# Row-by-row transfers for two early loads and the first store of an RMSNorm + SiLU kernel

**Chip and metric.** One core of one Trainium2 chip. The metric is the time of one execution on the device in microseconds (us).

## The reference

```python
batch, seq_len, hidden = 8, 1024, 2048            # x: 64 MB of float32, gamma: 2048
rms = np.sqrt(np.mean(x ** 2, axis=-1, keepdims=True) + eps)
out = gamma * x / rms
return (out * (1 / (1 + np.exp(-out)))).astype(np.float32)
```

## The kernel before

The engines go by the profile's names: PE multiplies matrices, DVE and ACT compute on vectors, SP only issues transfers here. A transfer (one `dma_start`) is cut into packets, which 16 DMA engines move (from 5 to 300 us 16.04 packets are open on the mean, by the packet records); a packet here is one contiguous run of 2 to 32 KB (a block's load is 128 packets of 32 KB, one a partition). When a transfer has landed, its completion semaphore says so, and that is what others wait on: load 0's was complete at 13.10, and the waits of ACT and DVE on it stand in the trace at 13.12 and 13.13.

The 8192 rows are cut into 16 blocks of 128 partitions x 4 rows (4 MB each, 32 KB in a partition). Six block buffers go round. Loads are issued from SP's queue, stores and gamma's 8 KB load from ACT's. The parts that matter:

```python
    J = 4
    BUFS, LEAD = 6, 6
...
    def load(b):
        xt = pool.tile([P, J * d], f32, name="xt")
        nc.sync.dma_start(out=xt, in_=xb[b])
        blocks[b] = xt
...
    def store(b):
        nc.scalar.dma_start(out=ob[b], in_=blocks[b])
        if b + LEAD < nblk:
            load(b + LEAD)
...
        grow = pool.tile([P, J * d], f32, name="xt")       # gamma's tile, one of the six buffers
        for b in range(BUFS - 1):
            load(b)                                        # loads 0 to 4
...
        nc.scalar.dma_start(out=grow[0:P:P // Q, 0:w], in_=...)   # gamma, on ACT's queue
        ...                                                # PE spreads gamma, DVE copies it to g
        load(BUFS - 1)                                     # load 5, into gamma's buffer
        ...
        sums(0)        # DVE squares rows 2 and 3, ACT rows 0 and 1
        invert(0)
        finish(0)      # DVE multiplies by 1/rms and g, ACT applies silu
        sums(1)
        invert(1)
        for b in range(1, last - 1):
            sums(b + 1, after_first=[b - 1])               # store(b - 1) is issued in here
            finish(b)
            invert(b + 1)
```

## Time and profile before

| | before |
|---|---|
| time, median of 3 runs | 317.5 us (317.2 to 317.74) |
| DVE and ACT busy | 71% each |
| loads + stores, share of 16 DMA engines | 49.7% + 49.2% |
| load 0 landed / store 0 issued / store 0 landed | 13.1 / 36.67 / 61.4 us |
| load 4 / load 5 landed | 64.6 / 84.0 us |
| last store issued / landed | 304.8 / 315.3 us |

The trace is of one further execution, which took 318.03 us.

The page's rows of slices cut the span into 40; the DMA row gives the busy share in tenths. A landing time here is the arrival of a transfer's completion in the trace. The prediction shows the lines themselves.

### The profile page before, as it was taken

How to read it: one execution, taken by the hardware profiler on the slowest of the kernel's cores; microseconds unless marked ns; L12 is line 12 of the kernel's file. 1: busy time of each engine (PE TensorE's matmuls, PEld its weight loads, DVE VectorE, ACT ScalarE, POOL GpSimd, SP SyncE). 2: the span in 40 equal slices, each digit the busy share in tenths (PEclk: the TensorE clock that was granted, in tenths of full speed). 3: DMA queues.
4: the chain of work that ended last, by engine and by line, in shares of the span. 5: the costliest groups of instructions: out<-in, count | busy, mean ns of one | idle time of the engine just before them, and what ended most of it. 6: DMA issues, size and time to landing. Idle time of an engine off the chain costs nothing.

```text
span 316.3 us, 444 instructions
## 1 busy us (share of the span) xinstructions
PE 2.1 (1%) x8; PEld 0.5 (0%) x8; DVE 223.5 (71%) x147; ACT 223.8 (71%) x144; POOL 0.2 (0%) x4
## 2 busy tenths in 40 slices
PE   0200000000000000000000000000000000000000
PEld 0000000000000000000000000000000000000000
DVE  0679499999493983939849397593966939993900
ACT  1357958999967777678676687676786776879540
POOL 0000000000000000000000000000000000000000
DMA  8999999999999999999999999999999999999996
GB/s 328 402 464 410 452 390 410 452 419 443 439 424 452 411 452 410 452 414 456 406 456 414 448 414 448 439 423 452 414 452 410 452 414 456 406 456 410 452 407 269
DMA packets 4763, 134.25 MB, mean 425 GB/s; under 512 B 532, under 2 KB 532, under 8 KB 536
## 3 DMA queue, kind: packets, MB, share of 16 engines
q1 hardware_dynamic: 2304, 67.11, 49.7%
q10 hardware_dynamic: 2456, 67.12, 49.2%
q14 instruction: 3, 0.02, 0.0%
HBM read 67.12 MB, written 67.11 MB: 424 GB/s over the span
## 4 chain that ended last, share of the span: by engine, by line
DMA 74%; DVE 14%; ACT 5%; issue 2%; DVEq 1%; ACTq 0%; SPq 0%
DMA xt<-in_x_dram 44%; DMA out_dram<-xt 30%; DVE xt L84 11%; ACT xt L88 3%; DVE junk_v L64 3%; ACT junk_a L68 1%; DVEq L164 1%; ACT L74 0%; ACT rms L74 0%; DVE rstd L79 0%; ACTq L93 0%; DVE ss L64 0%; SPq L52 0%; DVEq L64 0%; ACTq L74 0%
## 5 line engine op out<-in xcount | busy, mean ns | idle before, releaser
L84 DVE SCALAR_TENSOR_TENSOR xt<-xt,rstd,g 128x2048 f32<-128x2048 f32 x64 | 146.2, 2347 | 0.1
L88 ACT ACTIVATE xt<-xt 128x4096 f32<-128x4096 f32 x32 | 115.4, 3615 | 36.8 <-DVE xt L84 36.7
L64 DVE CUSTOM_DVE_ANT_0 junk_v<-xt 128x2048 f32<-128x2048 f32 x32 | 73.5, 2298 | 56.1 <-DMA xt<-in_x_dram 55.5
L68 ACT ACTIVATE junk_a<-xt 128x2048 f32<-128x2048 f32 x32 | 60.1, 1879 | 29.2 <-DMA xt<-in_x_dram 28.3
L74 ACT ACT_TABLE_LOAD x15 | 19.2, 1283 | 9.9 <-DVE ss L64 9.9
L88 ACT ACT_TABLE_LOAD x15 | 19.2, 1283 | 3.1 <-DVE xt L84 2.9
L79 DVE RECIPROCAL rstd<-rms 128x4 f32<-128x4 f32 x16 | 2.8, 172 | 11.3 <-ACT rms L74 11.3
L114 DVE COPY g<-junk_v 128x2048 f32<-128x2048 f32 x1 | 2.3, 2292 | 9.2 <-PE junk_v L112 9.2
L68 ACT ACTIVATION_READ_ACCUMULATOR junk_a<-xt 128x1 f32 x32 | 6.0, 186 | 0.0
L74 ACT ACTIVATE rms<-ss,eps_t 128x4 f32<-128x4 f32 x16 | 4.8, 297 | 1.2 <-DVE ss L64 1.1
L64 DVE DVE_READ_ACCUMULATOR2_ANT ss<- 128x1 f32 x32 | 4.5, 141 | 0.0
L112 PE MATMUL junk_v<-xt,ones 1*128 1x512 f32 x8 | 2.1, 1133 | 8.1 <-DMA xt<-in_gamma_dram 8.1
L107 ACT ACT_TABLE_LOAD x1 | 1.3, 1283 | 0.7 <-PEq L150 0.7
L105 DVE MEMSET ones<- 128x128 f32 x1 | 0.2, 165 | 0.8 <-PEq L150 0.8
L112 PEld LDWEIGHTS junk_v<-xt,ones 1*128 1x128 f32 x8 | 0.5, 306 | 8.1 <-issue 8.1
L107 ACT ACTIVATE junk_a<-ones 128x1 f32<-128x1 f32 x1 | 0.2, 174 | 0.0
L150 POOL MEMSET const-uint8-127<- 128x1 uint8 x1 | 0.1, 102 | 0.0
L150 POOL MEMSET const-bfloat16-1.0<- 128x1 bf16 x1 | 0.1, 101 | 0.0
L150 POOL MEMSET const-float32-0.0<- 128x1 f32 x1 | 0.1, 98 | 0.2 <-issue 0.2
L150 POOL MEMSET const-float32-1.0<- 128x1 f32 x1 | 0.1, 98 | 0.0
L106 DVE MEMSET eps_t<- 128x1 f32 x1 | 0.1, 59 | 0.0
## 6 DMA issues: line engine op xcount, KB each, us to landing
xt<-in_x_dram SPq DMA_DIRECT2D x16, 4096.0 KB, 42.0
out_dram<-xt ACTq DMA_DIRECT2D x15, 4096.0 KB, 35.2
out_dram<-xt ACTq DMA_DIRECT2D x2, 2048.0 KB, 10.4
xt<-in_gamma_dram ACTq DMA_DIRECT2D x1, 8.0 KB
```

The costliest lines, as they stand in the source:

```text
L64: nc.vector.tensor_tensor_reduce(out=junk_v, in0=row(b, j), in1=row(b, j), scale=1.0, scalar=0.0, op0=ALU.mult, op1=ALU.add, accum_out=ss[ ...
L68: nc.scalar.activation(out=junk_a, in_=row(b, j), func=ACT.Square, accum_out=ss[:, j:j + 1])
L74: nc.scalar.activation(out=rms, in_=ss, func=ACT.Sqrt, scale=1.0 / d, bias=eps_t)
L79: nc.vector.reciprocal(out=rstd, in_=rmss.pop(b))
L84: nc.vector.scalar_tensor_tensor(out=row(b, j), in0=row(b, j), scalar=rstds[b][:, j:j + 1], in1=g, op0=ALU.mult, op1=ALU.mult)
L88: nc.scalar.activation(out=blocks[b][:, cols], in_=blocks[b][:, cols], func=ACT.Silu)
L105: nc.vector.memset(ones, 1.0)
L107: nc.scalar.activation(out=junk_a[:, 0:1], in_=ones[:, 0:1], func=ACT.Square)
L112: nc.tensor.matmul(junk_v[:, c * w:(c + 1) * w], ones[k:k + 1, :], grow[k:k + 1, 0:w], start=True, stop=True)
L114: nc.vector.tensor_copy(out=g, in_=junk_v)
L150: nc = _bacc.Bacc("TRN2", target_bir_lowering=False, num_devices=1)
L164: with _tile.TileContext(nc) as tc:
```

## The change

Its intent: smaller runs for the transfers that meet at the start, so that the first store and the loads beside it take turns in smaller steps, and a block's rows come in one by one. The bytes and the compute stay the same.

```diff
+    LOADS, STORES = (3, 4), (0,)
...
+    def pieces(single):
+
+        step = d if single else J * d
+        return [slice(c, c + step) for c in range(0, J * d, step)]
+
     def load(b):
         xt = pool.tile([P, J * d], f32, name="xt")
-        nc.sync.dma_start(out=xt, in_=xb[b])
+        for c in pieces(b in LOADS):
+            nc.sync.dma_start(out=xt[:, c], in_=xb[b][:, c])
         blocks[b] = xt
...
     def store(b):
-        nc.scalar.dma_start(out=ob[b], in_=blocks[b])
+        for c in pieces(b in STORES):
+            nc.scalar.dma_start(out=ob[b][:, c], in_=blocks[b][:, c])
```

## The prediction

> **What bounds the kernel now.** I read the page's slices and queues first, then the timeline of the first 60 us and of the end, the waits of the issuing queues, and last the packet records behind the DMA view.
>
> ```profile
> span 316.3 us, 444 instructions
> ...
> DMA  8999999999999999999999999999999999999996
> GB/s 328 402 464 410 452 390 410 452 419 443 439 424 452 411 452 410 452 414 456 406 456 414 448 414 448 439 423 452 414 452 410 452 414 456 406 456 410 452 407 269
> ...
> q1 hardware_dynamic: 2304, 67.11, 49.7%
> q10 hardware_dynamic: 2456, 67.12, 49.2%
> ```
>
> q1 carries the loads, q10 the stores. Together they fill 98.9% of 16 engines' span; only the first and last slice are thin. By the packet records, data moves from 1.7 to 313 us (thinly to 314.9) with one packet at a time on each engine. A 32 KB packet takes 1213 ns, a 16 KB one 611, a 2 KB one 84. A block is 8 such packets per engine, and loads that run alone end 9.68 us apart; 16 blocks in and out are 32 x 9.68 = 309.8 us. So DMA bytes bind, and only idle DMA or dearer packets can change the time much.
>
> ```profile
> 0.73 139.01 SPq L52 DMA_DIRECT2D xt<-in_x_dram  x11
> ...
> 1.03 1.09 ACTq L108 DMA_DIRECT2D xt<-in_gamma_dram  x1
> 2.02 0.17 ACT L107 ACTIVATE junk_a<-ones 128x1 f32<-128x1 f32 x1
> ...
> 8.09 2.09 PE L112 MATMUL junk_v<-xt,ones 1*128 1x512 f32 x8 [8.09 <-DMA xt<-in_gamma_dram]
> 10.24 2.29 DVE L114 COPY g<-junk_v 128x2048 f32<-128x2048 f32 x1 [9.24 <-PE junk_v L112]
> 13.19 1.88 ACT L68 ACTIVATE junk_a<-xt 128x2048 f32<-128x2048 f32 x1 [10.99 <-DMA xt<-in_x_dram]
> 13.24 2.30 DVE L64 CUSTOM_DVE_ANT_0 junk_v<-xt 128x2048 f32<-128x2048 f32 x1 [0.71 <-DMA xt<-in_x_dram]
> ...
> 36.67 0.36 ACTq L93 DMA_DIRECT2D out_dram<-xt  x1
> ...
> 55.81 0.34 ACTq L93 DMA_DIRECT2D out_dram<-xt  x1
> ...
> 69.78 0.34 ACTq L93 DMA_DIRECT2D out_dram<-xt  x1
> ```
>
> In this timeline gamma's 8 KB go out on ACT's queue at 1.03, PE spreads them at 8.09, DVE copies them, and only then does DVE begin block 0 (13.24). The first store follows at 36.67. Until then six loads, 58 us of DMA work, keep the engines full. That cushion is what the start lives on.
>
> ```profile
> L93 ACTq DMA_DIRECT2D out_dram<-xt x4: 338/338/338, 69.8 to 123.4; - x4
> L93 ACTq EVENT_SEMAPHORE  x3: 17/17/17, 84.0 to 123.4; - x3
> ```
>
> These are the stores issued between 60 and 130 us: three of the four have an extra semaphore wait ahead of them, though no data need it. The trace's DMA instructions say why: every transfer names a completion semaphore, and there are eight, taken in turn in program order: 100, 102, 103, 104, 105 for loads 0 to 4, 106 for gamma, 108 for load 5, 109 for store 0, then 100 again for load 6. Store 3 is the next user of 106, and its extra wait is on 106, gamma's. Load 7, next on 103 after load 2, waits for 103 beside store 1's semaphore. So a transfer waits until the previous user of its semaphore has landed. Today that user landed long ago, and the wait takes 17 ns.
>
> [...] 1213 against 611 ns gives 9 ns plus 36.7 ns per KB, so about 310 ns for 8 KB. [...] once store 0 has begun, packets of q1 and q10 alternate. [...] here store 1's issue (55.81) comes as the last silu of block 1 ends, and nothing behind it overtakes it.
>
> **The change, part by part.**
>
> *Packets.* Three blocks go from 8 packets of 1213 ns to 32 of 310 on each engine: 3 x 8 x (4 x 310 - 1213) = 0.65 us at most. The start-to-start pitch is some 3 ns under the duration, so I take 0.5 us.
>
> *Numbering.* Loads 3 and 4 are now eight transfers, so the turns of the eight semaphores move. Loads 0 to 2 take turns 1 to 3, load 3's rows 4 to 7, load 4's first row 8; its other rows take turns 1, 2, 3 again and wait for loads 0, 1, 2 (harmless, the queue is full). **Gamma, the twelfth transfer, takes turn 4 again, and must wait until the first row of load 3 has landed.** That is my main step. Before, gamma was the sixth and waited for nobody.
>
> *When gamma goes.* Load 2 lands at 32.50; a row is 8 packets of about 0.306, 2.45 us, so ACT's queue is released at 34.95 and issues gamma at 35.0. Before, 5.1 us passed from issue to its first packet, of which about 1.2 is latency (load 0 took 1.0) and 3.9, some 3.2 packets of 32 KB, was queueing. Behind 8 KB packets that is about 1.0: first packet at 37.2, landed near 38.0, PE at 38.1, the copy done 4.4 later at 42.5 (8.09 to 12.53 before). DVE begins block 0 at 42.6 rather than 13.24: **29.3 us late**. ACT's squares of block 0, stuck behind the issue, start at 35 and are done before DVE needs them.
>
> *What it costs.* From there to the first store compute waits for no load, so I shift the timeline: stores 0, 1, 2 at 66.0, 85.1, 99.1. Loads: 3 ends at 42, 4 at 51.7, 5 (released when PE has read gamma at 40.2) at 61.4. Then the DMA has nothing.
> - Gap A: from 61.4 to the first store packet, 66.0 + 1.4 = 67.4: 6.0 us.
> - Gap B: store 0 alone runs from 67.4 to 77.2. Load 6 needs its buffer: landed 77.7, issued 77.8, first packet 78.9: 1.7 us.
> - Gap C: load 6 runs nearly alone until 88.6, then store 1 until 98.2; load 7 waits for it, first packet 99.8: 1.6 us.
>
> After that store 2 (99.1), 3 (113) and 4 (127), 14 us apart as compute runs, are ahead of the 19.36 us that a block takes in and out, so neither queue runs dry again. Loads 3 and 4 have long landed when store 0 goes out, so finer interleaving does nothing.
>
> *The end.* Stores lag and loads lead: I get load 14 at 256.7 (258.9 now), so compute (last issue 45.9 us after load 14) isn't the bound, and all lost DMA time stays lost. Sum: 6.0 + 1.7 + 1.6 + 0.5 = 9.8 us. 317.5 + 9.8 = **327.3 us**, 3.1% slower.
>
> **The rivals.**
>
> *No such wait for gamma* (a semaphore is picked by another rule than the turn, or the waits go another way). For it: today's trace shows no such wait between two transfers of different queues. Against it: the order of the eight is the turn throughout, 34 transfers long. Then the compute keeps its times, and the shares decide: store 0's 8 KB packets alternate with load 3's and 4's, but when store 0 is done near 58, about 3.5 us of load 4 is left against store 1's 32 KB packets, which get four fifths of the engines. Load 4 would land some 7 us late, and so the following loads. The end has about 3 us of slack (last store issued 304.8, landing 315.3, against 7.5 us that a half block takes by itself). 318 to 322 us.
>
> *Equal shares and no wait*: only the packets' 0.5 us; 318.0.
>
> *The gaps are smaller*: if gamma got through faster or store 0 came sooner, gap A shrinks one for one, but the 23.4 us of compute from block 0's start to its store stand in the timeline, and B and C are latency. I allow 2 us each way.
>
> *A gain*: the DMA is 98.9% busy and no packet gets cheaper; some 3 us at the two ends are all there is to win. I see no way to 2%.
>
> **Range and chances.** I give the gamma wait 85%, with a spread of about 2 us around 327.3; the rest lies at 318 to 322. Slower by over 2% begins at 323.9: 0.84; within 2% 0.15; faster 0.01. Range 323.5 to 329.5.
>
> **What would show it.** In the changed kernel's timeline gamma's issue stands near 35 instead of 1.03, PE's matmul near 38, DVE's first block near 42.6, store 0's first piece near 66; the slices have a hole near 62 to 67 and thin places near 78 and 99; the waits of ACT's first squares are some 24 us long beyond today's 11; queue shares sum to about 96%. If gamma is issued before 5 us, the main step is wrong. If gamma is late but no hole follows, the cushion of six loads was mis-sized.

In the trace of the kernel before, from 54 to 58 us, 30 packets of q1 stand against 29 of q10. That a transfer waits for the last user of its semaphore was inferred there from a few waits, such as store 3's on 106; the changed kernel and e8 show it below. The 1.2, 1.4 and 1.1 us before a first packet are my estimates (load 0's 1.00 us is what that trace shows on idle engines, and e4 later 0.86), and so are the 0.5 us from a last packet to its landing (0.43 at that kernel's end, from 314.89 to 315.32) and the 7.5 us of a half block (e1's last store took 7.20, from 307.82 to 315.02).

## The result

317.97 us (317.57 to 318.32, 6 runs) against 317.45 us (317.2 to 317.86, 6 runs) for the kernel before. The ratio is 1.0015, 95% interval 1.0002 to 1.0028. A ratio here is the mean time of one kernel's fast runs over that of the other's of the same rounds, so not quite the ratio of the medians. Executions over 1.5% slower than the fastest of the same kernel are left out of the means. The kernel is the same within 2%, and the forecast of 327.3 was wrong.

The page of the changed kernel, span, DMA slices, GB/s and queues:

```profile
span 316.0 us, 463 instructions
...
DMA  8999999999999999999999999999999999999996
GB/s 332 411 453 402 423 422 443 418 446 428 431 432 411 449 423 440 440 427 448 415 448 415 448 415 452 411 452 411 456 406 460 411 452 419 448 441 423 444 409 280
...
q1 hardware_dynamic: 3168, 67.11, 49.7%
q10 hardware_dynamic: 2888, 67.12, 49.3%
```

The DMA row is that of the kernel before: no hole anywhere. The packet counts grew by 864 and 432, which are the small runs (768 and 384 more packets) and the completions of the additional transfers (96 and 48 of 4 bytes). Yet the start of the changed kernel is not that of the kernel before. From its timeline (start, duration, engine, line, operation, and in brackets the idle time before it and what ended it):

```profile
12.96 1.09 ACTq L116 DMA_DIRECT2D xt<-in_gamma_dram  x1
14.09 1.88 ACT L75 ACTIVATE junk_a<-xt 128x2048 f32<-128x2048 f32 x1 [11.90 <-issue]
...
20.35 2.09 PE L120 MATMUL junk_v<-xt,ones 1*128 1x512 f32 x8 [20.35 <-DMA xt<-in_gamma_dram]
22.50 2.29 DVE L122 COPY g<-junk_v 128x2048 f32<-128x2048 f32 x1 [21.50 <-PE junk_v L120]
24.82 2.30 DVE L71 CUSTOM_DVE_ANT_0 junk_v<-xt 128x2048 f32<-128x2048 f32 x1
...
48.25 1.32 ACTq L101 DMA_DIRECT2D out_dram<-xt  x3
```

Gamma is late, as forecast, but at 12.96 and not at 35. By the operands that the trace keeps of each instruction, it waits on semaphore 100, load 0's, which was complete at 12.94. Compute starts 11.6 us later than before (24.82 against 13.24), and so does the first store (48.25 against 36.67). The transfers of both kernels take the eight completion semaphores in these turns, worked out from the semaphore that each transfer names in the trace:

| | turns 1 to 8 | then |
|---|---|---|
| before | loads 0 to 4, gamma, load 5, store 0 | load 6, store 1, ... |
| changed | loads 0, 1, 2, load 3's four rows, load 4's first row | **gamma**, load 4's other rows, load 5, store 0's rows, ... |

So there was a wait and a late start, and the DMA still never ran dry.

### The profile page after: what moved, and what is told of

The parts are those of the page before. It is cut to its first block, busy times and chain, and to the rows that moved or that the text cites. A ratio compares the mean times of both kernels' runs of the same rounds, so it can differ in the third digit from the quotient of the medians.

```text
span 316.0 us, 463 instructions
## 1 busy us (share of the span) xinstructions
PE 2.1 (1%) x8; PEld 0.5 (0%) x8; DVE 223.2 (71%) x147; ACT 223.1 (71%) x144; POOL 0.2 (0%) x4
## 4 chain that ended last, share of the span: by engine, by line
DMA 30%; ACT 21%; DVE 18%; another core or an unknown queue 12%; issue 11%; DVEq 1%; PE 1%; ACTq 0%; SPq 0%
DMA out_dram<-xt 15%; ACT xt L95 13%; DVE xt L91 13%; DMA xt<-in_x_dram 12%; DVE junk_v L71 4%; ACT junk_a L75 3%; DMA xt<-in_gamma_dram 2%; ACT L81 2%; ACT L95 2%; ACT rms L81 1%; DVE g L122 1%; DVEq L172 1%; PE junk_v L120 1%; ACTq L101 0%
## 5 line engine op out<-in xcount | busy, mean ns | idle before, releaser
L71 DVE CUSTOM_DVE_ANT_0 junk_v<-xt 128x2048 f32<-128x2048 f32 x32 | 73.5, 2296 | 36.7 <-DMA xt<-in_x_dram 36.1
```

The lines of the kernel that those rows point to most:

```text
L71: nc.vector.tensor_tensor_reduce(out=junk_v, in0=row(b, j), in1=row(b, j), scale=1.0, scalar=0.0, op0=ALU.mult, op1=ALU.add, accum_out=ss[ ...
```

## The experiments

Each experiment is one kernel, run in turn with the kernel before, whose median was 317.62 us beside e1 to e4, 317.54 beside e5, e6, e7 and e9, and 317.34 beside e8 and e10. Code cuts leave lines out where they show `...`. "Stretched" below is worked out from the trace's packet records: the sum of what all packets took beyond the usual duration of their size (1213, 611 and 309 ns for 32, 16 and 8 KB), divided by 16 engines. It is 1.69 us in the kernel before (0.77 of it at the very start, 0.85 between 37 and 42 us, almost all of it in the loads' packets between store 0's issue at 36.67 and its first packet at 40.76) and 1.38 us in the changed one.

My theory after the result (**the cushion**): gamma waits for the last user of its semaphore, and the six loads, which fill the DMA until about 61 us, hide the late start as long as store 0 goes out before that. **Rivals:** any late start is made up later; a late start costs the 0.5 us; the small packets and their share of the engines cost it.

### e1_rows_no_wait: the small packets without the wait

```diff
-        nc.sync.dma_start(out=xt, in_=xb[b])
+        if b in (3, 4):          # rows 0 and 2, then rows 1 and 3: 8 KB runs, two transfers
+            for k in range(2):
+                nc.sync.dma_start(out=halves(xt, k), in_=halves(xb[b], k))
+        else:
+            nc.sync.dma_start(out=xt, in_=xb[b])
...                               # store 0 alike
```

> Loads 3 and 4 and store 0 in 8 KB packets as in the change, but in two transfers each (rows 0 and 2, rows 1 and 3), so that the eight semaphores suffice for the first eight transfers and gamma waits for nobody. All theories: gamma issued near 1.0 us, DVE begins block 0 near 13.2, store 0 issued near 36.7. Packets only: 0.2 to 0.6 us over the kernel before (about 317.9), load 4 landed near 65 as before. Shares by packet (a 32 KB packet of store 1 for each 8 KB packet of load 4): load 4 landed at 69 to 74 instead of 64.6, the later loads some 5 us late too, and 320 to 322 us, because the end has only about 3 us of slack.

Measured: 317.89 us, ratio 1.0013 (1.0 to 1.0025). Gamma went out at 1.03, and DVE began block 0 at 13.18. The shares are by packet, as the transfers of the window from 62 to 66 us show (packets, MB, share of the engines; q10 has store 1's 32 KB packets, q1 mostly load 4's 8 KB ones):

```profile
q10 hardware_dynamic: 44, 1.41, 81.5%
q1 hardware_dynamic: 42, 0.47, 27.3%
```

About as many packets, three times the bytes. Load 4 landed at 68.3 instead of 64.6 and the last loads 3.05 us late. I had expected 5 us, and 320 us and more from it. Store 0's first packet came 4.4 us after its issue, no sooner than before (4.1), so it ended later, and when store 1's first packet went out at 60.6, 53 packets of load 4 were left, about 1.0 us of all engines' work, where the prediction had 3.5. The last store was issued at 307.82 instead of 304.77 and landed at 315.02 instead of 315.32: the slack at the end took all 3.05 us. So the time alone, which lies where "packets only" had it, would have misled; the landings decide.

### e2, e3, e4: gamma late by a chosen amount, all packets 32 KB

```diff
+        nc.scalar.copy(out=grow[0:1, 0:1], in_=blocks[0][0:1, 0:1])   # e3: blocks[1], e4: blocks[2]
         nc.scalar.dma_start(out=grow[0:P:P // Q, 0:w], ...)
```

> The kernel before, all 32 KB packets, with gamma made to wait for load 0 as it does in the changed kernel (one element of block 0 is copied into gamma's tile first). Theory of the cushion: gamma near 13.2, DVE begins block 0 at 24 to 26, store 0 near 48, no hole in the DMA slices, and the time of the kernel before within 0.3 us (317.2 to 317.8): the late start is free, and the change's 0.5 us are its packets. Rival, the late start costs the 0.5 us: 317.9 to 318.3.

> As the last, but gamma waits for load 1 (lands near 22.8). Theory of the cushion: DVE begins block 0 near 34.4, store 0 near 57.8, just before the six loads end near 61.5; no hole there, but a gap of 1.5 to 2 us while load 6 waits for store 0 near 71: 318.5 to 320 us. Rival, late compute is always made up: 317.5.

> As the last, but gamma waits for load 2 (lands near 32.5), which is 2.5 us earlier than the prediction had it wait in the changed kernel. Theory of the cushion, with the prediction's three gaps: DVE begins block 0 near 44, store 0 near 67.5, the DMA idle from about 61.5 to 69 and about 1.7 us twice after: 326.5 to 329.5 us. Rival, late compute is always made up: 317.5.

Measured: 319.08, 320.87 and 330.03 us, ratios 1.0053 (1.004 to 1.0065), 1.0101 (1.0086 to 1.0117) and 1.0397 (1.0383 to 1.0412). The page's DMA slices of e2_gamma_after_load0 and of e4_gamma_after_load2, and the stretches of e4's start (window, length, busy times, then clock, DMA share and GB/s at the end of the line):

```profile
DMA  8999999999999999999999999999999999999995
```

```profile
DMA  8999999378999999999999999999999999999996
```

```profile
52.00:61.00 9.00, 0.00 (x0) 0.00 (x0) 9.00 (x5) 4.87 (x2) 0.00 (x0) 1.00 0.95 408
61.00:68.00 7.00, 0.00 (x0) 0.00 (x0) 3.34 (x4) 6.95 (x6) 0.00 (x0) 1.00 0.00 0
68.00:77.50 9.50, 0.00 (x0) 0.00 (x0) 8.53 (x7) 6.37 (x8) 0.00 (x0) 1.00 1.03 442
77.50:80.00 2.50, 0.00 (x0) 0.00 (x0) 2.50 (x2) 1.69 (x1) 0.00 (x0) 1.00 0.72 197
```

There are the gaps A and B of the prediction: 7 us with no transfer at all, because the six loads have landed and store 0 isn't out until 67.33, and a second dip while load 6 waits for store 0. From the packet records, A is 7.4 us, B 1.6 and C only 0.6, where the prediction had 6.0, 1.7 and 1.6. "Always made up" falls. The cushion holds for the holes, but not wholly: all three times missed their ranges. e2 has no hole and still lost 1.5 us, above the range of its rival too (to 318.3), and e3 (range to 320) and e4 (to 329.5) came out above theirs. The rest is stretched packets: 2.37 us in e2, 3.20 in e3, 4.84 in e4, mostly close after a queue starts beside the other or again after it was empty. In e2 the last packet ended at 316.54, against 314.89 in the kernel before; that is the whole of the difference of the two traced executions (319.65 and 318.03 us).

What stretching costs can be seen in the GB/s, the last number of a stretch. e2_gamma_after_load0, then the changed kernel, whose compute starts as late:

```profile
45.00:60.00 15.00, 0.00 (x0) 0.00 (x0) 10.41 (x10) 11.01 (x13) 0.00 (x0) 1.00 0.97 400
60.00:75.00 15.00, 0.00 (x0) 0.00 (x0) 14.97 (x10) 14.00 (x10) 0.00 (x0) 1.00 1.05 452
75.00:90.00 15.00, 0.00 (x0) 0.00 (x0) 14.97 (x11) 14.91 (x10) 0.00 (x0) 1.00 0.98 400
```

```profile
45.00:60.00 15.00, 0.00 (x0) 0.00 (x0) 10.41 (x10) 11.01 (x13) 0.00 (x0) 1.00 1.02 434
60.00:75.00 15.00, 0.00 (x0) 0.00 (x0) 14.96 (x10) 14.00 (x10) 0.00 (x0) 1.00 1.04 442
75.00:90.00 15.00, 0.00 (x0) 0.00 (x0) 14.96 (x11) 14.91 (x10) 0.00 (x0) 1.00 0.99 420
```

### e5_all_rows_8k: the price of the packets

```diff
+    D = d + 16                                   # rows 64 bytes further apart on chip
...
-        nc.sync.dma_start(out=xt, in_=xb[b])
+        nc.sync.dma_start(out=xt[:, :, 0:d], in_=xb[b])      # one transfer, 8 KB runs; stores alike
```

> Every block in and out in 8 KB packets, one transfer each (rows stand 64 bytes further apart on chip, so that a transfer's runs can't be joined); semaphores, order and compute as in the kernel before, gamma early. It measures the packets alone, 32 blocks of them where the change has 3. Packet theory, from 309 against 1213 ns (23 ns for each 32 KB and 8 of them an engine and block): 0.18 us a block, 32 x 0.18 = 5.9 us, so 322.5 to 324 us, with shares and landings as before because all packets are alike. Rival, the pitch between packets is less than their records say: 318 to 321 us.

Measured: 321.08 us, ratio 1.0108 (1.0089 to 1.0126). The packet records would make it 5.9 us; it is 3.54 us (321.08 - 317.54) for 32 blocks, **0.11 us a block**, so 0.33 us for the change's three. The records overlap a little more when packets are small, as the rival had it (their sum grew by 5.5 us an engine, the end of the last packet by 3.2), though the time is a little above the rival's numbers. It is an upper bound: e5's first packet also comes 0.38 us later (2.11 instead of 1.73), once and not per block.

### e6, e7, e10: the parts alone

```diff
-    LOADS, STORES = (3, 4), (0,)
+    LOADS, STORES = (3, 4), ()       # e6_loads_only
+    LOADS, STORES = (), (0,)         # e7_store_only; e10: this, and e2's copy ahead of gamma
```

> The change without its store part: gamma waits for load 0 as in the changed kernel, store 0 is one 32 KB transfer and starts beside load 5, as in e2_gamma_after_load0. If store 0's 8 KB packets are what kept the late start from costing the 1.5 us that it cost with 32 KB packets: 318.9 to 319.9 us, about 0.7 us more of stretched packets (records well over 1213 ns) at 49 to 52 and near 75 to 90. Rival, the eight load pieces are what kept it: 317.8 to 318.3.

> The change without its load part: gamma early (1.0), store 0 in four row transfers from 36.7 against 32 KB loads. Shares by packet: store 0 gets a fifth of the engines, its last row lands near 71 instead of 61.4, load 5 near 67 instead of 84; the load queue is empty for some us after that. DMA without a hole: 317.7 to 318.7 us, the upper end if the load queue's new start costs as much as in e2. Rival, equal shares: landings as before, 317.8.

> e2_gamma_after_load0 with store 0 in four row transfers, all loads 32 KB. Late gamma cost 1.5 us with one 32 KB store 0 (e2) and about 3 (of wide spread) with that and the load pieces (e6), but no more than 0.2 in the changed kernel. If store 0's small packets are what spares it (load 5 then ends some 7 us before store 0, not with it): 317.6 to 318.1 us. Rival, it takes the load pieces too: 318.8 to 319.5.

Measured: e6 320.63 us over six runs; the five fast ones spread from 318.6 to 323.0 with the median at 319.06, ratio 1.0084 (1.0038 to 1.013); e7 317.8, ratio 1.0005 (0.9992 to 1.0018); e10 317.72, four runs from 317.51 to 317.75 and two at 319.08 and 320.05, ratio 1.0033 (1.0009 to 1.0056). In e7 the shares by packet are as forecast: store 0's last row landed at 71.5 and load 5 at 67.2.

So the load part alone makes the kernel slower, since it brings gamma's wait, and unsteady, which that wait alone doesn't explain (e2's runs lie within 0.7 us); the store part alone costs nothing that these runs can tell from zero; and with the late gamma, store 0's small packets spare most of the cost in four of e10's six runs. The other two lost more than e2, and the intervals of e10 and e2 overlap; so that these packets are enough by themselves is likely, not shown. That they are needed is clearer: all six runs of the changed kernel (to 318.32) lie below every run of e6 (from 318.6), which lacks only them. With them load 5 lands at 64.4 to 64.7 and store 0 at 71.6 to 71.8 (e10 and the changed kernel); without them both land at 72 (e2, e6). After that the stretched packets between 75 and 90 us are 0.05 us in e10, 0.31 in the changed kernel, 0.86 in e2 and 1.28 in e6. These traces are of a spared run of e10 (317.51) and of one of e6's faster ones (318.78). Why a packet stretches there isn't shown, and e10 has 0.6 us of it at 60 to 62 with no queue starting; that stays open, as do e10's two longer runs and e6's spread.

### e8_loads_234: moving gamma's turn

```diff
-    LOADS, STORES = (3, 4), (0,)
+    LOADS, STORES = (2, 3, 4), (0,)
```

> The change with block 2's load in rows too, nothing else. In the built program gamma now takes the twelfth semaphore turn, after eleven loads, and so comes behind load 2's second row (in the changed kernel it came ninth, behind load 0). That row should land near 27.7. If a transfer always waits for the last user of its semaphore: gamma near 27.8, DVE begins block 0 near 38 to 39.5, store 0 near 62, a hole of 2 to 3 us from about 61.5, two gaps near 1.5, stretched packets and 0.44 us for four blocks of small packets: 322 to 326 us. Rival, the wait in the changed kernel had to do with load 0 itself: gamma near 13, DVE near 25, 318 to 318.5.

Measured: 324.24 us, ratio 1.0217 (1.0203 to 1.0231). From its timeline:

```profile
27.72 1.09 ACTq L116 DMA_DIRECT2D xt<-in_gamma_dram  x1
...
37.89 2.30 DVE L71 CUSTOM_DVE_ANT_0 junk_v<-xt 128x2048 f32<-128x2048 f32 x1
...
61.31 1.82 ACTq L101 DMA_DIRECT2D out_dram<-xt  x3
```

Load 2's second row was complete at 27.70 and gamma went out at 27.72. The wait follows the semaphore's last user, whichever it is; the rival falls. The time lies in the range, but not by the holes expected: 0.7 us at 61 (2 to 3 expected), 1.9 at 72 and 0.4 from 95 on (two of 1.5 expected). One more block in rows turns a kernel within 0.2% into one 2.2% slower, by the turn of a semaphore.

### e9_gamma_after_row_of_load3: the prediction's own case

```diff
+        nc.scalar.copy(out=grow[0:1, 0:1], in_=blocks[3][0:1, 0:1])   # in the changed kernel
         nc.scalar.dma_start(out=grow[0:P:P // Q, 0:w], ...)
```

> The changed kernel with gamma made to wait for the first row of load 3, as the prediction had it (one element of that row is copied into gamma's tile first). The prediction's sum: gamma near 35.0, DVE begins block 0 at 42.6, gaps 6.0 + 1.7 + 1.6 us, 327.3. Corrected by what the first four runs showed (the queueing ahead of gamma doesn't shrink with the packets, so DVE begins near 46.5 and store 0 goes out near 70; each new start of a queue stretches packets): a hole from 61.5 to 71, 330 to 333 us. Rival, the changed kernel makes up any late start: 318.

Measured: 331.69 us, ratio 1.0442 (1.0425 to 1.0458). From its timeline, and the stretch of the hole:

```profile
35.16 1.09 ACTq L117 DMA_DIRECT2D xt<-in_gamma_dram  x1
42.50 2.29 DVE L123 COPY g<-junk_v 128x2048 f32<-128x2048 f32 x1 [41.50 <-PE junk_v L121]
44.83 2.30 DVE L71 CUSTOM_DVE_ANT_0 junk_v<-xt 128x2048 f32<-128x2048 f32 x1
```

```profile
61.50:69.50 8.00, 0.00 (x0) 0.00 (x0) 3.76 (x4) 7.95 (x6) 0.00 (x0) 1.00 0.06 27
```

With gamma where I had put it, the hole that I had predicted is there, and the time is even 4.4 us above my number. It lies in the corrected range, though DVE began earlier than corrected (44.83, not 46.5).

### All of them side by side

"Idle" is the time with packets missing after the start, from the packet records; "stretched" is against the 1.69 us of the kernel before; packets at 0.11 us a block. Measured is the difference of the medians of the same rounds. Each trace is one execution, up to 0.6 us off its kernel's median (before 318.03, changed 317.78, e2 319.65, e4 330.63), so a sum and a measured time can differ by as much.

| | gamma out | store 0 out | idle | stretched | packets | sum | measured |
|---|---|---|---|---|---|---|---|
| changed | 12.96 | 48.25 | 0 | -0.3 | 0.3 | 0.0 | 0.5 |
| e2 | 13.21 | 48.36 | 0 | 0.7 | 0 | 0.7 | 1.5 |
| e3 | 23.07 | 57.83 | 2.1 | 1.5 | 0 | 3.6 | 3.3 |
| e8 | 27.72 | 61.31 | 2.9 | 3.1 | 0.4 | 6.4 | 6.9 |
| e4 | 32.61 | 67.33 | 9.4 | 3.2 | 0 | 12.6 | 12.4 |
| e9 | 35.16 | 68.25 | 9.9 | 3.4 | 0.3 | 13.6 | 14.2 |

The sums are means over engines, while the time is set by the engine that ends last; in e2 that makes up the other 0.8 us (the last 16 packets end 0.9 us later on the mean than in the kernel before, the very last 1.65). None of the experiments points to a version that beats the kernel before, which leaves some 3 us outside its DMA work.

## Why the prediction was wrong

- **What binds** was right: DMA bytes (loads and stores fill 98.9% of the engines' span in the kernel before, 99.0% in the changed one). Where there is a hole, its size and the time go together (e3, e8, e4, e9).
- **That gamma would have to wait** was right, and with it that ACT's first squares are stuck behind it (idle 11.90 us behind the issue). At 12.96 this cost them little: before, they began at 13.19, now at 14.09.
- **The step that failed** is "Gamma, the twelfth transfer, takes turn 4 again, and must wait until the first row of load 3 has landed." Gamma took the ninth turn and came behind load 0. I had counted turns in the order of the source. The kernel before can't tell that order from the built program's, as every transfer there stands in the same place in both. In every kernel here that cuts load 4 (changed, e1, e6, e8, e9) gamma's turn comes straight after load 4's first piece, before the rest of it. It isn't that pieces which have to wait go behind gamma: in e1 none of load 4 has to wait, and in e8, where gamma has the twelfth turn, three pieces that have to wait come before it. Which rule decides, no run shows.
- **What followed from it:** "29.3 us late" was 11.6. Store 0 went out at 48.25, before the loads ran out at about 61, so gaps A, B and C of 9.3 us never opened. With store 0 behind the loads' end they open (e4, e9). The cushion itself was rightly sized: the prediction has the loads end at 61.4, and e4's hole begins at 61.
- **The sum, had gamma waited for load 3**, was 4.4 us too small (e9). Compute began at 44.83 and not 42.6, because the way from gamma's issue to PE shrank less behind small packets than I took it to: from issue to the first matmul it was 5.2 us (the copy, 42.50, less 2.15, less 35.16), where I had 3.1. The idle time was 9.9 us for 9.3, near by luck: gap A was 7.9 us and not 6.0, B 1.6 for 1.7, but C only 0.4 for 1.6, as store 2 was out (101.4) before store 1 had landed (102.7). The stretched packets, 3.4 us, weren't in my sum at all.
- **Packets:** 0.5 us predicted; at most 0.33 by e5. The prediction's "36.7 ns per KB" is per 1000 bytes; for KB as used here it is 37.6. Its 310 ns for 8 KB is right (309).
- **The rivals:** "no such wait" was given 318 to 322. Its share mechanism is right (e1, e7), its size was not: loads 3.05 us later where it had about 7, all within the slack that the prediction named. "Equal shares and no wait" has 318.0, the measured number, by reasons that don't hold: there is a wait, and shares are by packet. Its number is luck.
- **The end:** "stores lag and loads lead" holds. The changed kernel's last load landed at 270.8 instead of 278.2, for load 5 took four of five bytes from store 0. The transfers of both queues in the changed kernel from 54 to 58 us:

```profile
q1 hardware_dynamic: 47, 1.54, 89.1%
q10 hardware_dynamic: 47, 0.39, 22.7%
```

47 packets each, 1.54 MB against 0.39.

So the time of the changed kernel is the kernel before plus 0.5 us (interval 0.1 to 0.9). About 0.3 of it are packets, by e5's rate; the rest is too small for these runs to place. As far as the runs show, two effects of the change nearly cancel: the load part's late gamma (1.5 us by itself, e2), and the store part's small packets, with which most of that cost is spared (changed against e6; e10 in four runs of six).

## What to carry to other kernels

Splitting a transfer also uses up completion semaphores (here loads 3 and 4 took eight turns instead of two, and gamma went out at 12.96 instead of 1.03): count how many are in flight, and look in the built program at whose semaphore the next small but urgent transfer, here gamma, has to wait for. In this kernel a late start of compute was cheap as long as enough loads were queued to reach the first store (from e2 to e3 store 0 goes out 9.5 us later, for 1.8 us), and cost about one for one beyond that (from e3 to e4 again 9.5 us later, for 9.2 us). Before a wait is priced, its place in the built order has to be read and not inferred from the source.

## What the runs show of the transfers

- With runs of 8 and 32 KB the queues took turns run by run: from 54 to 58 us 47 runs of 32 KB against 47 of 8 KB (changed), so 4 to 1 in bytes; with equal sizes 30 against 29 of 32 KB (before) and 105 against 105 of 8 KB (e1).
- Load 0 took 1.00 us from issue to first packet (before) and store 0 0.86 on idle engines (e4), but store 0 beside a busy load queue 4.1 (before), 3.5 (changed) and 4.4 (e1), the last two with 8 KB packets in service.
- A further packet cost little: e5's 0.11 us a block over 24 more packets an engine is 4.6 ns each at most. A packet's duration in the trace overstates it (309 x 4 - 1213 = 23 ns for three more packets).
- Packets stretched about a queue's start: 0.85 us in the kernel before between 37 and 42 us, and over the whole run 3.1 to 3.4 us more than that kernel in e4, e8 and e9.
- The eight completion semaphores were used again in turn, and gamma's transfer waited for the last user of its own: it went out at 12.96 (changed; load 0 complete at 12.94) and 27.72 us (e8; load 2's second row at 27.70) instead of 1.03.
